# A hybrid decoder layer on one core: other distances between the steps of a hand-written TensorE order

## The chip, the core and the metric

The kernel runs on one core of one Trainium2 chip. Its metric is device time in microseconds (us), the median of several runs. A core has TensorE (PE in the rows; its weight loads are PEld) for matrix products into PSUM, VectorE (DVE), ScalarE (ACT) and GpSimd (POOL) for elementwise work, and SyncE (SP), whose queue here issues every DMA.

## The reference

One layer. `h` is the RMS-normalised input (1024 tokens of 1024 channels), `p = h @ W_in` holds the columns of all branches. Branch A is dilated sliding-window attention in three head groups, merged by their softmax denominators. Branch B is RWKV-7 time mixing: eight heads of 64 channels, each with a 64 by 64 state that is updated token by token:

```python
state = (state * w_t[:, :, None, :] + sa[..., None] * b_t[:, :, None, :]
         + v_t[..., None] * k_t[:, :, None, :])
y = jnp.einsum('bhvk,bhk->bhv', state, r_t)
...
y_rwkv = (o_rwkv * jax.nn.silu(z_rwkv)) @ w_up_rwkv[l]
merged = jax.nn.sigmoid(g_attn) * y_attn + jax.nn.sigmoid(g_rwkv) * y_rwkv
out = merged @ w_out[l]
x = x + rms_norm(out, post_norm_gain[l])
```

## The kernel before

Large products are made of three fp32r products each (high by high, high by low, low by high half). The program has four stages: `start` (normalise and transpose the input), `rwkv` (the recurrence), `attention` and `finish`.

In `rwkv` the tokens are cut into 8 segments of 128, each of two chunks of 64, and the heads into 4 pairs. For each segment there are four pieces of work, written as generators that stop (`yield`) between steps:

- `rwkv_prep` (11 steps): load and shift k and r; **wa**, the product of the low-rank codes (`pg<-wa,waup`), then the decay on DVE (`sig`, a scan into `c`); **hs,q**, the squared norms of k (`pg<-hs,q`), then `rn` on DVE (L549) and a power on POOL (L550); the **rn transpose** on PE (`pg<-ident,rn`), copied by DVE into `rt` (L560); **selp** (`pg<-rt,selp`), which spreads `rt` again, read by DVE (`kk`, L573); two steps of **ar,bk** products (`pg<-ar,bk`, 64 rows each), masked into `gt` by DVE (L597). After the second, `rwkv_blocks` writes the 16 by 16 diagonal blocks to DRAM (`tin_d`), loads them back as `xinv`, and inverts them on DVE: the **chain**, 28 small dependent operations of L624 and L626. Its result goes to DRAM (`x_d<-xinv`, four DMAs) and comes back as `xd` (`xd<-x_d`, two DMAs), and DVE transposes it into **xt** (L646). Four steps of small products (`pi`, the first three of them also followed by DVE or ACT work) then finish the inverse.
- `rwkv_rows` (3 steps): two transposes of `bw`, and `v` with `r,blk`.
- `rwkv_chain` (6 steps, C in the tables): per chunk hop 1 (`rhs<-uv,gt`, `rhs<-state,ar`, copied to `rhs_s`), hop 2 (`upd<-rhs_s,tt`, copied to `uv` by DVE L731 and ACT L732) and hop 3 (`snew<-uv,bkt`, `rhs<-uv,gt`, added to the state by DVE L738). This is the recurrence proper: each hop needs the one before.
- `rwkv_post` (2 steps): group norm and output.

Between these steps PE is given **fill**: products of projections that the rest of the program needs (`acc<-hh,whi` and its like), taken from one iterator: the second half of r/k/v, the RWKV gate (`z_chunks`), the merge gate of branch B, and the first EARLY of the 8 tiles of the other merge gate. A step of fill is one 512-column product, or two of 256 columns while r/k/v last. The other tiles of that gate are computed in `finish`.

The order of PE in this stage is fixed by hand (`keep_in_program_order`, L145). PROLOGUE is a list of (step, steps of fill behind it), where "0", "1", "2" are the preparations of the first three segments and "f" the rows of the first. LOOP is the list for one segment i: C is the chain, `t` the last step of the preparation of segment i, `e` that of i+1 (steps 8 to 10), `a` that of i+2 (steps 2 to 7), `b` the first of i+3, `f` the rows of i+1, `h` the post of i-1; its number is multiplied by FILLS (6 for most segments). All other engines and SP have an in-order queue whose order a scheduler sets at build time from its own estimate of times; so a new order on PE also gives new orders there.

PSUM for the preparation's products (`pg`) has two buffers; `raw` (loaded k, r, v) has two.

Of the kernel before, what the change touches and what calls it, by code (L numbers as in the profile page):

```python
# [34 lines left out]
C = 64  # L35
# [3 lines left out]
HALF = 512  # L39
YB = 2  # L40
BVB = 2
EARLY = 2

PROLOGUE = (("0", 24), ("0", 10), ("0", 10), ("0", 8), ("0", 44), ("0", 4), ("0", 4), ("1", 12), ("1", 16), ("1", 12),
            ("f", 4), ("f", 4), ("1", 8), ("1", 24), ("0", 8), ("0", 8), ("0", 8), ("1", 4), ("1", 6), ("0", 6), ("2", 0),
            ("f", 8))
LOOP = (("C", 0), ("t", 0), ("f", 1), ("a", 1), ("h", 1), ("C", 0), ("f", 1), ("a", 2), ("C", 0), ("a", 1), ("h", 2),
        ("C", 0), ("a", 1), ("f", 0), ("e", 2), ("C", 2), ("a", 1), ("e", 0), ("C", 1), ("a", 1), ("e", 1), ("b", 0))  # L50
FILLS = 6 * [6] + [5, 3]
CPS = SEG // C
KAPPA = math.exp(-0.5)
# [59 lines left out]
class Kernel:  # L113
# [233 lines left out]
    def rwkv(self):  # L347
# [5 lines left out]
        with ExitStack() as ctx:  # L353
# [53 lines left out]
            for t0 in range(0, S, 512):  # L407
# [11 lines left out]
            spans, fill = self.span_chunks(0), itertools.chain(self.span_chunks(1), self.z_chunks(), (  # L419
                self.gate(d, 1) for d in range(KT)), (self.gate(d, 0) for d in range(EARLY)))  # L420
            first, fill = self.ahead(spans[:8]), self.ahead(spans[8:] + list(fill))
# [11 lines left out]
            rows = self.rwkv_rows(0)  # L433
            for g, n in PROLOGUE:
                next(rows if g == "f" else prep[int(g)])
                run(n)
            for i in range(NSEG):
# [3 lines left out]
                work = dict(t=prep[i], e=prep[i + 1], a=prep[i + 2], b=prep[i + 3], f=rows, h=post)  # L441
                for g, n in LOOP:
                    if g == "C":
# [587 lines left out]
    def finish(self):  # L1031
        nc, tc, a = self.nc, self.tc, self.a
        with ExitStack() as ctx:
# [3 lines left out]
            whole, orw = self.whole, self.orw  # L1037
            for d in range(EARLY, KT):
                for _ in self.gate(d, 0):
# [122 lines left out]
```

## Time and profile before

| | |
|---|---|
| median of 3 runs | 1431.96 us (1424.61 to 1434.63) |
| the profiled execution | 1427.3 us, of which the span 1425.5 us |
| PE busy | 1334.2 us (94% of the span) |
| DVE, ACT, POOL busy | 55%, 40%, 33% |
| recurrence, fixed order | about 97 to 540 us of the span |

A row of the timeline has: start in us, length in us, engine, line, operation, tile written and tiles read, shape, count, and in brackets how long the engine stood idle before it and what ended that. A matrix product of two fp32 operands shows twice its count. PE's ends are modelled, so the length of a product is longer than the distance to the next.

### The profile page before, as it was taken

How to read it: one execution, taken by the hardware profiler on the slowest of the kernel's cores; microseconds unless marked ns; L12 is line 12 of the kernel's file. 1: busy time of each engine (PE TensorE's matmuls, PEld its weight loads, DVE VectorE, ACT ScalarE, POOL GpSimd, SP SyncE). 2: the span in 40 equal slices, each digit the busy share in tenths (PEclk: the TensorE clock that was granted, in tenths of full speed). 3: DMA queues.
4: the chain of work that ended last, by engine and by line, in shares of the span. 5: the costliest groups of instructions: out<-in, count | busy, mean ns of one | idle time of the engine just before them, and what ended most of it. 6: DMA issues, size and time to landing. Idle time of an engine off the chain costs nothing. (4 is left out here: it accounts for less than half of the span.)

```text
span 1425.5 us, 25770 instructions
## 1 busy us (share of the span) xinstructions
PE 1334.2 (94%) x10078; PEld 1118.8 (78%) x10078; DVE 780.5 (55%) x1675; ACT 575.4 (40%) x1378; POOL 477.4 (33%) x378
## 2 busy tenths in 40 slices
PE   4998799999999999999989998999899999998997
PEld 3898799777777777888868886888678877776886
DVE  5302755656565433465686558754776577338523
ACT  4435665654665332254426433543344320003211
POOL 1335534643453333322132223222223234434300
PEclk9998899999999999999999999999999999999999
DMA  8583444323332222111131112111221145654216
GB/s 170 156 241 103 119 103 120 98 71 80 106 80 57 77 77 86 46 35 52 36 96 46 41 47 75 54 50 37 58 74 31 40 150 176 201 168 141 73 35 172
DMA packets 199230, 131.17 MB, mean 92 GB/s; under 512 B 52788, under 2 KB 179340, under 8 KB 199108
## 3 DMA queue, kind: packets, MB, share of 16 engines
q1 hardware_dynamic: 199108, 129.52, 33.0%
q8 instruction: 79, 1.29, 0.4%
q14 instruction: 43, 0.35, 0.1%
HBM read 100.31 MB, written 33.89 MB: 94 GB/s over the span
## 5 line engine op out<-in xcount | busy, mean ns | idle before, releaser
L142 PE MATMUL acc<-hh,whi 128*128 128x512 f32 (+1 forms) x1360 | 480.0, 376 | 24.8 <-DVE kl L862 10.9
L142 PE MATMUL acc<-hh,wlo 128*128 128x512 f32 (+1 forms) x1360 | 469.8, 369 | 2.0 <-POOL wlo L138 1.9
L142 PE MATMUL acc<-hl,whi 128*128 128x512 f32 (+1 forms) x1360 | 469.8, 369 | 0.0
L138 POOL TENSOR_TENSOR wlo<-wstage,whi 128x512 fp32r<-128x512 f32 x186 | 250.8, 1349 | 532.2 <-DVE whi L135 262.2
L142 PEld LDWEIGHTS acc<-hh,whi 128*128 128x128 f32 x1360 | 247.7, 192 | 70.8 <-issue 16.9
L142 PEld LDWEIGHTS acc<-hh,wlo 128*128 128x128 f32 x1360 | 247.6, 192 | 41.1 <-POOL wlo L138 3.7
L142 PEld LDWEIGHTS acc<-hl,whi 128*128 128x128 f32 x1360 | 247.5, 192 | 35.3 <-issue 1.7
L882 ACT ACTIVATE L<-L,nm 128x128 f32<-128x128 f32 (+1 forms) x192 | 83.9, 438 | 84.6 <-DVE nm L879 84.4
L876 DVE CUSTOM_DVE_ANT_0 L<-pw,bias 128x128 f32<-128x128 f32 (+1 forms) x192 | 62.4, 350 | 51.6 <-PE pw L875 51.1
L861 POOL CAST k<-k 64x512 fp32r<-64x512 f32 x48 | 47.4, 988 | 107.0 <-ACT k L860 98.4
L135 DVE CAST whi<-wstage 128x512 fp32r<-128x512 f32 x108 | 53.2, 494 | 50.7 <-PE acc L142 32.3
L860 ACT CAST k<-acc 64x512 fp32r<-64x512 f32 x48 | 42.9, 894 | 75.4 <-DVE kl L862 51.9
L137 ACT CAST whi<-wstage 128x512 fp32r<-128x512 f32 x78 | 48.4, 621 | 61.0 <-PE acc L142 28.8
L852 ACT ACTIVATE q<-acc 64x512 fp32r<-64x512 f32 x48 | 43.9, 914 | 57.8 <-DVE q L853 28.6
L862 DVE TENSOR_TENSOR kl<-acc,k 64x512 fp32r<-64x512 f32 x48 | 45.7, 952 | 33.8 <-ACT k L860 33.4
L624 DVE TENSOR_TENSOR xtmp<-xinv 64x14 f32<-64x14 f32 (+6 forms) x112 | 33.5, 299 | 44.4 <-DMA xinv<-tin_d 41.5
L853 DVE SCALAR_TENSOR_TENSOR q<-acc,q 64x512 fp32r<-64x512 f32 x48 | 44.8, 933 | 20.9 <-ACT q L852 20.1
L952 ACT CAST ph<-pw 128x512 fp32r<-128x512 f32 x72 | 40.8, 583 | 36.0 <-PE pv L961 19.4
L953 DVE TENSOR_TENSOR pl<-pw,ph 128x512 fp32r<-128x512 f32 x72 | 47.2, 670 | 11.7 <-ACT ph L952 10.4
L875 PE MATMUL pw<-kl,q 128*128 128x128 f32 (+1 forms) x192 | 50.6, 278 | 1.4 <-DVE kl L862 1.4
L1102 PE MATMUL acc<-wo,mh 128*128 128x512 f32 x128 | 49.8, 389 | 0.0
L1103 PE MATMUL acc<-wo,mh 128*128 128x512 f32 x128 | 49.8, 389 | 0.0
(229 smaller groups left out, 2173.3 us busy)
## 6 DMA issues: line engine op xcount, KB each, us to landing
wstage<-in_w_in_dram SPq DMA_DIRECT2D x170, 256.0 KB
x<-in_x_dram SPq DMA_DIRECT2D x32, 256.0 KB
raw<-raw_d SPq DMA_DIRECT2D x24, 258.0 KB
raw_d<-rv SPq DMA_DIRECT2D x24, 256.0 KB
wb<-wd SPq DMA_DIRECT2D x24, 256.0 KB
bias_d<-bias_r SPq DMA_DIRECT2D x24, 192.0 KB
tb_d<-tb SPq DMA_DIRECT2D x16, 256.0 KB
ga_d<-tb SPq DMA_DIRECT2D x16, 256.0 KB
```

Of the source, the lines that this page charges most:

```text
L135: self.nc.vector.tensor_copy(hi, x)
L137: self.nc.scalar.copy(hi, x)
L138: self.nc.gpsimd.tensor_tensor(lo, x, hi.bitcast(F32), ALU.subtract)
L142: ins = self.nc.tensor.matmul(*args, **kw)
L861: nc.gpsimd.tensor_copy(self.gview(ks2[h][b], g, half), hi.bitcast(F32))
L862: nc.vector.tensor_tensor(self.gview(kl[h][a], g, half), pv, hi.bitcast(F32), ALU.subtract)
L875: nc.tensor.matmul(ps[:, :w], qs2[h][:, qc], kl[h][:, kc], start=False, stop=True)
L876: nc.vector.tensor_tensor_reduce(l[:, l0:l0 + w], ps[:, :w], self.bias[h][:, bo:bo + w], 1.0, -3.0e38, ALU.add, ALU.max, st[:, gi, 0, h, n ...
L882: nc.scalar.activation(ls, ls, AF.Exp, bias=nm[:, n:n + 1], scale=1.0, accum_out=st[:, gi, 1, h, n:n + 1])
L953: nc.vector.tensor_tensor(pl[:, :cw], ps[:, :cw], ph[:, :cw].bitcast(F32), ALU.subtract)
L1102: nc.tensor.matmul(ps, mh[k][:, ts], wh[:, k], start=k == 0, stop=False)
L1103: nc.tensor.matmul(ps, mh[k][:, ts], wl[:, k], start=False, stop=False)
```

## The change

Three tables of numbers change. EARLY goes from 2 to 3, so one more tile of the second merge gate is in the fill of the recurrence and one fewer is in `finish` (48 products of 512 columns). PROLOGUE spends 268 steps of fill instead of 232, at other places. LOOP spends the same 18 units per segment in another order, and moves `wa` in front of the first `bw`, `ar,bk` in front of `pi`, the second `ar,bk` directly behind hop 3, and the load of `b` ahead.

```diff
-EARLY = 2
+EARLY = 3
...
-PROLOGUE = (("0", 24), ("0", 10), ("0", 10), ("0", 8), ("0", 44), ("0", 4), ("0", 4), ("1", 12), ("1", 16), ("1", 12),
+PROLOGUE = (("0", 40), ("0", 16), ("0", 12), ("0", 8), ("0", 32), ("0", 8), ("0", 8), ("1", 24), ("1", 14), ("1", 12),
...
-        ("C", 0), ("a", 1), ("f", 0), ("e", 2), ("C", 2), ("a", 1), ("e", 0), ("C", 1), ("a", 1), ("e", 1), ("b", 0))
+        ("C", 0), ("a", 1), ("f", 1), ("e", 1), ("C", 0), ("b", 1), ("a", 0), ("e", 2), ("C", 0), ("a", 1), ("e", 2))
```

TensorE in the loop, segment 3, from the first chunk's hop 2 to the rn transpose (the fill between is left out). Before:

```order
L142 MATMUL upd<-rhs_s,tt_436 64x64 x8
L148 MATMUL pg<-ident,bw 128x128 x4
...
L142 MATMUL pg<-hs,q 128x2 x4
...
L142 MATMUL snew<-uv,bkt 64x64 x8
L142 MATMUL rhs<-uv,gt_432 64x64 x8
L148 MATMUL pg<-ident,rn 8x128
```

And now:

```order
L142 MATMUL upd<-rhs_s,tt_436 64x64 x8
...
L148 MATMUL pg<-ident,bw 128x128 x4
...
L142 MATMUL pg<-hs,q 128x2 x4
...
L142 MATMUL snew<-uv,bkt 64x64 x8
L142 MATMUL rhs<-uv,gt_432 64x64 x8
...
L148 MATMUL pg<-ident,rn 8x128
```

Each "..." is six steps of fill, but twelve between hs,q and snew before. From the segment's first hop to the rn transpose there are 36 steps of fill before and 42 now; from the rn transpose to selp 18 and now 12.

VectorE at the same place, from the end of the chain of L624 and L626 on. Before:

```order
L624 TENSOR_TENSOR xtmp<-xinv 64x14
L626 TENSOR_TENSOR xinv<-xinv,xtmp 64x14
L549 TENSOR_SCALAR rn<-pg 128x8
L493 SCALAR_TENSOR_TENSOR zt<-zt,acc 128x512
L556 COPY wc<-q 128x8
L738 TENSOR_TENSOR state<-snew,sw 128x256
L560 COPY rt<-pg 8x128
L646 STREAM_TRANSPOSE xt<-xd 128x512
```

And now:

```order
L624 TENSOR_TENSOR xtmp<-xinv 64x14
L626 TENSOR_TENSOR xinv<-xinv,xtmp 64x14
L731 COPY uv<-upd 64x4x64
L646 STREAM_TRANSPOSE xt<-xd 128x512
L549 TENSOR_SCALAR rn<-pg 128x8
L556 COPY wc<-q 128x8
L738 TENSOR_TENSOR state<-snew,sw 128x256
L560 COPY rt<-pg 8x128
```

The transpose of `xd`, which comes back from DRAM after the chain, stood behind `rn`, `state` and `rt`; now it stands ahead of them, and so does the copy `uv` stand behind the chain (before, seven of its operations came after `uv`). The same turn, xt ahead of rn, is in the queue in segments 0 to 4; in segment 5 rn stays ahead, and segments 6 and 7 have no rn.

VectorE in the prologue, around the rn and rt of the second preparation. Before:

```order
L626 TENSOR_TENSOR xinv<-xinv,xtmp 64x5x10
L549 TENSOR_SCALAR rn<-pg 128x8
L624 TENSOR_TENSOR xtmp<-xinv 64x54
...
L624 TENSOR_TENSOR xtmp<-xinv 64x14
L626 TENSOR_TENSOR xinv<-xinv,xtmp 64x14
L560 COPY rt<-pg 8x128
```

And now:

```order
L624 TENSOR_TENSOR xtmp<-xinv 64x44
L549 TENSOR_SCALAR rn<-pg 128x8
L626 TENSOR_TENSOR xinv<-xinv,xtmp 64x11x4
...
L624 TENSOR_TENSOR xtmp<-xinv 64x14
L626 TENSOR_TENSOR xinv<-xinv,xtmp 64x14
L560 COPY rt<-pg 8x128
```

Here `rt` stays behind the whole chain, and `rn` moves from behind 10 of its 28 operations to behind 21. On PE there are 86 steps of fill between the second ar,bk of the first preparation and the selp of the second, instead of 60.

The attention stage has the same order on every engine as before; in `finish` one gate tile is gone from PE, DVE, POOL and SP, and nothing else is moved on PE.

## Rows read from the trace of the kernel before

**Rows 1.** The page's part 1: busy us (share), instructions; PE alone.

```profile
PE 1334.2 (94%) x10078; PEld 1118.8 (78%) x10078; DVE 780.5 (55%) x1675; ACT 575.4 (40%) x1378; POOL 477.4 (33%) x378
```

**Rows 2.** Waits of PE, 0 to 560 us: releaser, us in total, times, longest.

```profile
PE pg L142 <- ACT q L542: 8.6, 2, 5.8
PE pg L148 <- POOL rn L550: 7.6, 6, 1.9
PE pg L142 <- DVE rt L560: 5.4, 1, 5.4
PE pg L142 <- DVE kk L573: 2.2, 2, 1.9
...
PE snew L142 <- ACT uv L732: 0.9, 2, 0.6
```

**Rows 3.** Timeline of PE in the prologue, 100 to 166 us.

```profile
112.52 1.87 PE L142 MATMUL pg<-hs,q 128*128 128x2 f32 x8 [5.76 <-ACT q L542]
...
115.25 0.63 PE L142 MATMUL acc<-hh,wlo 128*128 128x256 f32 x2
...
149.27 0.94 PE L142 MATMUL pg<-hs,q 128*128 128x2 f32 x7 [2.81 <-ACT q L542]
...
165.66 2.07 PE L142 MATMUL pg<-rt,selp 8*128 8x128 f32 x8 [5.35 <-DVE rt L560]
```

**Rows 4.** Busy time by stretch, the prologue: engines, then granted clock, DMA share, GB/s.

```profile
97.00:195.00 98.00, 83.62 (x929) 79.28 (x929) 42.49 (x89) 54.18 (x129) 48.19 (x39) 0.90 0.46 119
```

**Rows 5.** Timeline of DVE in segment 3 of the loop.

```profile
348.75 0.17 DVE L624 TENSOR_TENSOR xtmp<-xinv 64x14 f32<-64x14 f32 x1 [3.99 <-DMA xinv<-tin_d]
...
360.33 0.18 DVE L626 TENSOR_TENSOR xinv<-xinv,xtmp 64x14 f32<-64x14 f32 x1
360.43 0.15 DVE L549 TENSOR_SCALAR rn<-pg 128x8 f32<-128x8 f32 x1
...
367.60 0.71 DVE L646 STREAM_TRANSPOSE xt<-xd 128x512 f32<-128x512 f32 x1 [3.52 <-DMA xd<-x_d]
```

**Rows 6.** Timeline of PE in segment 3: hop 1, hop 3, rn transpose.

```profile
344.02 1.11 PE L142 MATMUL rhs<-uv,gt 64*128 64x64 f32 x16
...
359.57 0.69 PE L142 MATMUL snew<-uv,bkt 128*64 128x64 f32 x16
...
362.34 0.27 PE L148 MATMUL pg<-ident,rn 128*8 128x128 f32 x1 [1.47 <-POOL rn L550]
```

**Rows 7.** SP's DMA issues behind the chain of segment 2.

```profile
310.77 1.80 SPq L629 DMA_DIRECT2D x_d<-xinv  x4
313.94 1.28 SPq L644 DMA_DIRECT2D xd<-x_d  x2
```

**Rows 8.** Segment 0: PE's rn transpose, then DVE's xt and rt.

```profile
212.25 0.27 PE L148 MATMUL pg<-ident,rn 128*8 128x128 f32 x1 [0.97 <-POOL rn L550]
...
214.97 0.71 DVE L646 STREAM_TRANSPOSE xt<-xd 128x512 f32<-128x512 f32 x1 [4.33 <-DMA xd<-x_d]
...
215.92 0.26 DVE L560 COPY rt<-pg 8x128 f32<-8x128 f32 x1
```

**Rows 9.** Timeline of PE: a 64-row product alone among fill.

```profile
132.62 0.40 PE L142 MATMUL acc<-hl,whi 128*128 128x256 f32 x2
132.94 1.21 PE L142 MATMUL pg<-ar,bk 64*64 64x64 f32 x64
134.08 0.51 PE L142 MATMUL acc<-hh,wlo 128*128 128x256 f32 x2
134.43 0.41 PE L142 MATMUL acc<-hh,whi 128*128 128x256 f32 x2
134.67 0.41 PE L142 MATMUL acc<-hl,whi 128*128 128x256 f32 x2
```

**Rows 10.** Waits of PE in the last stage, 1100 to 1426 us.

```profile
PE acc L142 <- DVE tb L467: 6.3, 4, 2.8
```

**Rows 11.** What DVE waited for before L646, whole span: us, times.

```profile
  DMA xd<-x_d: 32.3, 8
```

More of the change, by code (lines that the diff above doesn't have):

```diff
@@ L41 @@
 BVB = 2
-EARLY = 2
-PROLOGUE = (("0", 24), ("0", 10), ("0", 10), ("0", 8), ("0", 44), ("0", 4), ("0", 4), ("1", 12), ("1", 16), ("1", 12),
-            ("f", 4), ("f", 4), ("1", 8), ("1", 24), ("0", 8), ("0", 8), ("0", 8), ("1", 4), ("1", 6), ("0", 6), ("2", 0),
+EARLY = 3
+PROLOGUE = (("0", 40), ("0", 16), ("0", 12), ("0", 8), ("0", 32), ("0", 8), ("0", 8), ("1", 24), ("1", 14), ("1", 12),
+            ("f", 4), ("1", 20), ("f", 4), ("1", 16), ("0", 8), ("0", 8), ("0", 8), ("1", 6), ("1", 6), ("0", 6), ("2", 0),
             ("f", 8))
-LOOP = (("C", 0), ("t", 0), ("f", 1), ("a", 1), ("h", 1), ("C", 0), ("f", 1), ("a", 2), ("C", 0), ("a", 1), ("h", 2),
-        ("C", 0), ("a", 1), ("f", 0), ("e", 2), ("C", 2), ("a", 1), ("e", 0), ("C", 1), ("a", 1), ("e", 1), ("b", 0))
+LOOP = (("C", 0), ("t", 0), ("a", 1), ("f", 1), ("h", 1), ("C", 1), ("f", 1), ("a", 1), ("C", 1), ("a", 1), ("h", 1),
+        ("C", 0), ("a", 1), ("f", 1), ("e", 1), ("C", 0), ("b", 1), ("a", 0), ("e", 2), ("C", 0), ("a", 1), ("e", 2))
 FILLS = 6 * [6] + [5, 3]
```

## The prediction

> **What bounds the kernel now.** I read the busy shares first. TensorE is busy 94% of the span [rows 1], and the change adds and removes no product, so only the time in which PE stands still, or runs at the lower clock, can change: 91 us of standing in all. The waits of PE up to the end of the recurrence come next [rows 2]: 8.6 us for `q`, 7.6 for `rn` in six waits, 5.4 for `rt`, 2.2 for `kk`, 0.9 for `uv`. The timeline of the prologue [rows 3] shows that `q` and `rt` are three long waits: 5.76, 2.81 and 5.35 us, 13.9 together. Behind such a wait products are slower: a pair of 256 columns takes 0.63 us at 115.25 [rows 3] against 0.40 at 132.62 [rows 9], and the granted clock is 0.90 over these 98 us [rows 4]. If that is a mix of the two levels, 1.2 and 2.4 GHz, about 20 us ran at the lower one, which loses at most 9.8 us. Part of the 20 us was standing anyway; I take 7.3, or 2.4 per long wait, with 0 and 3.3 as ends. Last I read the loop: what VectorE does between the chain, `rn` and `xt` [rows 5, 8], where that lies against PE's steps [rows 6], and what SP does meanwhile [rows 7].
>
> **The prologue.** All distances here are in fill steps of 0.24 us: so far apart do undisturbed pairs start, 134.43 to 134.67 [rows 9]. First wait: from the loads to hs,q there are 22 more steps (16 and 6), 5.3 us of the 5.76; 0.5 us stays. Second: 10 more steps from loads to hs,q, 2.4 of 2.81; 0.4 stays. Third, the selp that waits for `rt`: `rt` still stands behind the whole chain in VectorE's queue. PE now has 26 more steps before it, 6.2 us, but no longer loses the second wait and the slow clock behind it, 5.2 us, so it arrives only 1.0 us later against the chain: 4.3 us stay, split between `rn`, which has moved back to the 21st of 28 operations, and `rt`. With 2.4 us of slow clock that makes 7.6 of the 21.2 us before: **13.6 us saved**. Ends: 21.2 (all waits gone) and 0 (the chain or GpSimd's queue holds the ar,bk products up instead).
>
> **The loop, VectorE's queue.** Here the price lies. In segments 0 to 4 `xt` now stands ahead of `rn`. `xt` needs `xd`, which goes to DRAM and back after the chain's last operation: 360.51 to 367.60, 7.09 us [rows 5]. It waits for that DMA in all eight segments [rows 11]. The engine does not pass over a waiting operation: in segment 0, where `xt` already stood ahead of `rt`, PE's rn transpose was through at 212.5, yet `rt` ran at 215.92, right behind `xt` [rows 8]. And PE's rn transpose waits for `rn` and the power on GpSimd: 360.43 to 362.34, 1.91 us [rows 5, 6].
>
> For one segment, in us after its hop 1 (344.02 [rows 6]): the chain runs from 4.73 to 16.49 [rows 5]. Its ar,bk now comes six steps sooner before the next hop 1, up to 1.4 us, but the masks stay behind `state` and the norm's sums on VectorE; I take 0.9, so it ends at 15.6. `xd` is back at 22.7, `xt` done at 23.4, and the rn transpose can start at 25.3. PE arrives there at 18.32 less the 1.47 it waited, plus six steps (1.4) and one more change of product shape (0.2): 18.4. **It waits 6.9 us**, where it waited 1.5. The copy `uv`, now behind the chain, holds hop 3 until 16.0 against an arrival near 15.6; that is inside the 6.9. The wait is long like the three of the prologue, so 2.4 us of slow clock follow. Segment 0 from its own rows: `xt` done at 215.68, transpose at 217.6, arrival 212.25 less 0.97 plus 1.6, so 4.7 and 2.4 [rows 8]. Segment 5 keeps `rn` ahead, and with 12 more steps between ar,bk and `rn` waits nothing.
>
> Sum: 4 x (6.9 + 2.4) + 7.1 = 44.3, less the 7.6 and 0.9 of before [rows 2]: **35.8 us lost**. Ends: if the chain ends 3 us sooner and no clock falls, 4 x 3.9 + 2 - 8.5 = 9; if it ends 2 us later, with 3.3 us of clock, 4 x 12.2 + 8 - 8.5 = 48. Behind the waiting `rn` stand `wc`, `state` and `rt`. `state` is wanted at the next hop 1, twelve steps behind the transpose, and is done before the transpose: no further wait. From the rn transpose to selp there are six steps fewer, 1.4 us, so `kk` may be late for r,blk; the slow fill there gives these steps back, and I leave `kk` at 2.2.
>
> By the Trainium skill, DMA: Bandwidth & Descriptors, Anatomy of one DMA, a DMA costs about 2 us whatever its size; two in turn would be 4.0 us, an estimate, and the wait 3.8 instead of 6.9. The trace speaks against stopping there: between the two landings SP also issues, 1.80 and 1.28 us [rows 7], which is the missing 3.1; the row's 7.09 stands.
>
> **Shapes side by side.** A 64-row product alone among fill costs 0.32 - 0.24 us on entry and 0.35 - 0.24 on exit, 0.2 together [rows 9]. Each loop pass has two such groups fewer (wa behind `pi`, ar,bk before `pi` and behind hop 3, against pi now apart from r,blk): 0.4 us. But four 128-row steps (two `bw`, rn, r,blk) stood next to a hop or `pi` and now have a change of their own, about 0.1 each. Zero, with 3 us either way over the eight segments.
>
> The Trainium skill, TensorEngine Tiling (Array Packing), Key Properties, says that a change of tiling mode drains the engine. These rows agree that it costs something, but by it the order would be a gain only if changes went away, and they mostly move.
>
> **The gate tile.** 48 products leave the last stage and 36 steps enter the prologue, 12 the end of the recurrence, at about 0.24 us: nothing, to 0.4 us. In the last stage four waits for `tb` [rows 10] come from VectorE's other work; the tile that goes stands behind them, so I leave them. If that cover is gone, the next stage's first products meet VectorE's work earlier: 3 us at most, the longest of these waits.
>
> **Sum.** 1427.3 - 13.6 + 35.8 + 0.4 = 1449.9: **1450 us**. The profiled execution is 4.7 us below the median of the runs, 1431.96, so the same sum against the median would be 1454; both are in the range.
>
> **Rivals.**
> - *The two halves meet* (0.18): the chain ends three or four us sooner, because sooner `wa` takes `sig` and the scan out of its way, and no clock falls. Loss 9 to 20, prologue -13.6: about 1430. For it, 3.99 us of idle time before the chain [rows 5]; against it, the trip of `xd`, which nothing shortens. A trip of 4.0 us would give 5 x 3.1 = 15.5 less, 1434, the same case.
> - *The prologue gives nothing* (0.14): GpSimd's order or `rn` makes new waits as long as the old ones. 1427.3 + 35.8: 1463.
> - *Faster* (0.08): the loop's wait does not grow. The chain's loads land early, while PE is in hop 1, and it ends within 10 us of that hop; then `xt` is done at 17.8 and the transpose waits 1.3 us, as today. Each us later costs 5. With all 21.2 us of the prologue saved, and the loop as before or a little worse (+5): 1411. For it, VectorE idles for these loads; against it, they wait for two DMAs of their own that the change leaves alone.
> - *Nothing moves* (0.04): PE's longer waits fall where other engines would have stopped it anyway: 1427.
>
> The forecast has 0.56, its own range 1438 to 1462. With the first two rivals, and the ends of the prologue and the loop, 1428 to 1468 leaves out 0.2: the fast side mostly. A measurement of this kernel tells about 1% (14 us) from no change. Above 1446 lie 0.48 of the forecast and the second rival's 0.14: slower 0.62. Same: 0.08 of the forecast, 0.16 of the first rival, 0.04: 0.28. Faster 0.10.
>
> **What would show it.** In the trace after: five waits of PE's rn transpose of 5 to 8 us each in segments 0 to 4, none in segment 5; VectorE idle 5 us or more before `xt`, with `rn` directly behind; a granted clock below 1.0 in those segments; in the prologue no wait of 3 us for `q`, and one of some 4 us for `rn` or `rt`. Wrong would be: `rn` waits of 2 us or less (then the chain or the trip was misjudged), a prologue still at 0.90, or a last stage longer by over 3 us.

## The result, and the profile after

The changed kernel takes 1445.4 us (median of 6 runs, 1441.5 to 1449.4) against 1426.0 for the kernel before on the same chip (six runs, among them the three behind the 1431.96 of the table above): a ratio of 1.0124, with an interval from 1.0101 to 1.0147. The loss is clear of the noise, but small. The profiled run has a span of 1444.3 us, 18.8 more than before.

PE was busy for about as long as before and stood still more [rows 1]:

```profile
PE 1339.4 (93%) x10078; PEld 1120.2 (78%) x10078; DVE 767.7 (53%) x1673; ACT 578.6 (40%) x1380; POOL 477.7 (33%) x378
```

Where the time went is read from marks on PE, the same instructions in both traces: the first hop 1 of segment 0, that of segment 6, and the last hop of the recurrence; then the first product of the attention stage that has to wait. Before (timeline of PE):

```profile
194.87 1.11 PE L142 MATMUL rhs<-uv,gt 64*128 64x64 f32 x16
...
488.01 1.11 PE L142 MATMUL rhs<-uv,gt 64*128 64x64 f32 x16
...
543.87 0.69 PE L142 MATMUL snew<-uv,bkt 128*64 128x64 f32 x16
...
568.82 0.47 PE L142 MATMUL acc<-hh,whi 128*128 128x512 f32 x1 [2.52 <-DVE q L853]
```

After, with segment 3 between them (its hop 1, first bw, rn transpose and post transpose, with what PE waited for in brackets):

```profile
191.89 1.11 PE L142 MATMUL rhs<-uv,gt 64*128 64x64 f32 x16
...
356.80 1.11 PE L142 MATMUL rhs<-uv,gt 64*128 64x64 f32 x16
...
365.55 0.66 PE L148 MATMUL pg<-ident,bw 128*128 128x128 f32 x4 [2.88 <-ACT sig L530]
...
381.44 0.37 PE L148 MATMUL pg<-ident,rn 128*8 128x128 f32 x1 [3.36 <-POOL rn L550]
381.47 0.78 PE L142 MATMUL acc<-hh,whi 128*128 128x512 f32 x1
...
384.18 0.86 PE L148 MATMUL pg<-ident,d 128*128 128x128 f32 x4
...
518.93 1.11 PE L142 MATMUL rhs<-uv,gt 64*128 64x64 f32 x16
...
574.83 0.69 PE L142 MATMUL snew<-uv,bkt 128*64 128x64 f32 x16
...
600.49 0.47 PE L142 MATMUL acc<-hh,whi 128*128 128x512 f32 x1 [0.53 <-DVE q L853]
```

- Prologue: the first hop comes 3.0 us sooner, with 36 more fill steps of 0.24 us ahead of it (8.6): 11.6 us saved in this pair of traces.
- Segments 0 to 5, the same fill in both: 293.1 us before, 327.0 after: **33.9 us lost**.
- Segments 6 and 7, the same fill in both: 55.9 us in both.
- From the last hop to the end: 881.6 and 869.5, 12.1 less. 48 products have left `finish`, and 12 of them run behind the last hop (102 products up to the wait of the last row, 90 before), so 36 products of 0.24 us are 8.6 of it: **3.5 saved**. 2.0 of that is the first wait of the attention stage, 2.52 us before and 0.53 after: the 12 steps cover it.

Together that makes +18.8 us. What ended PE's waits in the loop (190 to 580 us of after; releaser, us in total, times, longest):

```profile
PE pg L148 <- ACT sig L530: 13.9, 5, 3.9
PE pg L148 <- POOL rn L550: 13.5, 5, 4.1
PE pg L142 <- DVE kk L573: 4.0, 2, 2.2
PE pi L142 <- DVE xq L652: 3.6, 3, 2.1
```

The wait for `rn` grew from 7.6 to 13.5 us [rows 2], but as much went to a waiter that was not there before: the bw transposes wait for `sig`. VectorE in the same segment 3 (in brackets its idle time and what ended it):

```profile
361.05 0.17 DVE L624 TENSOR_TENSOR xtmp<-xinv 64x14 f32<-64x14 f32 x1 [6.67 <-DMA xinv<-tin_d]
...
363.12 0.68 DVE L756 TENSOR_TENSOR d<-yt,sm 128x512 f32<-128x512 f32 x1
...
371.56 0.17 DVE L626 TENSOR_TENSOR xinv<-xinv,xtmp 64x14 f32<-64x14 f32 x1
371.65 0.41 DVE L731 COPY uv<-upd 64x256 f32<-64x256 f32 x1
378.91 0.71 DVE L646 STREAM_TRANSPOSE xt<-xd 128x512 f32<-128x512 f32 x1 [6.85 <-DMA xd<-x_d]
379.55 0.13 DVE L549 TENSOR_SCALAR rn<-pg 128x8 f32<-128x8 f32 x1
```

And ScalarE:

```profile
363.83 0.63 ACT L757 ACTIVATE yt<-d 128x512 f32<-128x512 f32 x1 [3.61 <-DVE d L756]
364.37 1.13 ACT L530 ACTIVATE sig<-pg,vecs 128x128 f32<-128x128 f32 x4
```

The lower half is the forecast: 6.85 us of idle time before `xt`, and `rn` directly behind it, where it ran right behind the chain before [rows 5]. The upper half is the same pattern twice in a row: the chain's first operation waits for its load, the post's `d` stands behind it on VectorE, `yt` waits for `d` on ScalarE, and `sig` stands behind `yt`. `wa` now comes ahead of the first bw and has filled both `pg` buffers; until `sig` has read one, the bw transpose can't start.

The granted clock, [rows 4] and a stretch of segment 1, the loop's slowest segment (busy time by stretch of after; the number behind the five engines is the clock):

```profile
97.00:195.00 98.00, 91.45 (x1052) 87.02 (x1051) 39.50 (x97) 57.07 (x134) 52.93 (x42) 0.95 0.48 128
...
245.00:295.00 50.00, 43.35 (x476) 34.79 (x474) 27.61 (x68) 25.56 (x66) 20.07 (x16) 0.90 0.28 74
```

### The profile page after: what moved, and what is told of

Same layout as the page of the kernel before. It is cut to its first block, busy times and chain, and to the rows that moved or that the text cites. A ratio compares the mean times of both kernels' runs of the same rounds, so it can differ in the third digit from the quotient of the medians.

```text
span 1444.3 us, 25775 instructions
## 1 busy us (share of the span) xinstructions
PE 1339.4 (93%) x10078; PEld 1120.2 (78%) x10078; DVE 767.7 (53%) x1673; ACT 578.6 (40%) x1380; POOL 477.7 (33%) x378
## 5 line engine op out<-in xcount | busy, mean ns | idle before, releaser
L142 PE MATMUL acc<-hh,whi 128*128 128x512 f32 (+1 forms) x1360 | 485.3, 380 | 23.9 <-DVE kl L862 11.3
L135 DVE CAST whi<-wstage 128x512 fp32r<-128x512 f32 x106 | 53.0, 501 | 46.8 <-PE acc L142 27.9
L624 DVE TENSOR_TENSOR xtmp<-xinv 64x14 f32<-64x14 f32 (+6 forms) x112 | 29.2, 261 | 46.3 <-DMA xinv<-tin_d 43.7
```

Source lines behind the costliest of these rows:

```text
L135: self.nc.vector.tensor_copy(hi, x)
L142: ins = self.nc.tensor.matmul(*args, **kw)
```

## The experiments

Theory: the transpose `xt`, which waits for the trip of `xd`, stands ahead of `rn`, and sets when PE gets through the rn transpose; the wait for `sig` lies inside the same stretch and only takes some of it over. Rival: two separate causes whose prices add. The first three runs change VectorE's or ScalarE's queue; PE's order in all of them is that of the changed kernel. Each edit is a pin: `issue_after` puts one instruction behind another in its engine's queue, and the scheduler orders the rest around it. A ratio compares with the kernel before run beside the same experiment on the same chip, where its median lay between 1427.5 and 1430.4 us; between experiments the ratios are the safer comparison. 1445.4 us is a ratio of 1.0124.

**E1: xt behind rt again (segments 1 to 6).**

```diff
-        nc.vector.tensor_copy(rt, ps[0:n, 1])
+        self.rt_at = nc.vector.tensor_copy(rt, ps[0:n, 1])
...
-        nc.vector.transpose(flat(dt), flat(d))
...
+        if not 1 <= sg["s"] <= 6: nc.vector.transpose(flat(dt), flat(d))
...
+        if 1 <= sg["s"] <= 6:
+            with self.tc.issue_after(self.rt_at.ins): nc.vector.transpose(flat(dt), flat(d))
```

> The changed kernel (1445.4 us), with only one thing different: on VectorE the transpose xt of segments 1 to 6 stands behind rn, state and rt again. Theory (the trip of xd ahead of rn is what PE waits for): PE's rn transpose finds rn ready about 17.3 us after hop 1 (chain end 14.9, uv, rn, power 1.9) and arrives later than that, held up by the waits for sig, so the 13.5 us of rn waits in the loop go, with some 5 us of slow clock; the 13.9 us for sig stay: 1427 us. Rival (the chain itself, not the trip, makes rn late): rn waits of 1.5 us or more stay in each segment and the time is 1436 or more. Other rival: xt is now late for pi, a new wait of the same size: 1440 or more.

Measured 1426.0 us, a ratio of 0.997 (0.995 to 0.999). The waits for `rn` in the loop are gone altogether, those for `sig` stay (190 to 580 us, first rows):

```profile
PE pg L148 <- ACT sig L530: 14.7, 5, 4.1
PE pi L142 <- DVE xq L652: 4.4, 5, 1.6
```

Up to the last hop nothing but `xt` has another place in the queues of VectorE, ScalarE and GpSimd than in the changed kernel. So the trip, not the chain, made `rn` late, and `pi` has room for the later `xt`.

**E2: sig ahead of yt (segments 1 to 5), xt left ahead of rn.**

```diff
-                nc.scalar.activation(dst[:, p], ps[:, p], AF.Tanh, bias=col(b0, p), scale=0.5)
+                self.aa_at = nc.scalar.activation(dst[:, p], ps[:, p], AF.Tanh, bias=col(b0, p), scale=0.5)
...
-        nc.scalar.activation(yt, dh, AF.Square)
+        with self.tc.issue_after(self.aa_at.ins): nc.scalar.activation(yt, dh, AF.Square)
```

> The changed kernel, with only the post's square yt (L757) put behind sig and aa (L530) in ScalarE's queue in segments 1 to 5; xt stays ahead of rn. Theory (one bound for the stretch from hop 1 to the rn transpose: chain, then xd, then rn, 24.4 us): the five waits for sig, 13.9 us, go, but the rn waits grow by as much in segments 1 to 4, from 11.0 to some 21 us; only segment 5, which has rn ahead, keeps its 3.9 us: 1439 to 1442 us. Rival (two causes that add): the rn waits stay at 13.5 and the time falls by 13.9 and 4 to 6 us of slow clock, to about 1426.

Measured 1444.3 us against 1445.4, a ratio of 1.009 (1.006 to 1.011) against 1.0124: 1 us faster by the medians, 5 by the ratios, where the intervals overlap. The waits for `sig` are gone; others took their place:

```profile
PE pg L148 <- POOL rn L550: 16.6, 5, 4.3
PE pg L142 <- ACT bkt L688: 4.8, 3, 2.6
PE pi L142 <- DVE xq L652: 3.9, 4, 2.1
PE pg L142 <- DVE kk L573: 2.9, 3, 1.5
PE pg L142 <- DVE rt L560: 1.2, 1, 1.2
```

The rival, which asked for some 19 us, is out. The time is 2 us above the theory's range: part of the room went to hs,q, which waits for `bkt`, and segment 5, where `xt` stands ahead of `rt` instead of `rn`, still takes 50.6 us.

**E3 and E11: both edits.**

> Both edits in one: xt behind rt, sig ahead of yt. Theory: no wait for sig, rn waits of about 1 us per segment as in the kernel before, the loop at some 293 us for segments 0 to 5 instead of 327: 1410 to 1414 us, below the kernel before (1426) by what the prologue saved. Rival (the order on PE itself costs, shapes or clock): the waits go but the loop keeps 10 us or more of the loss: 1422 or more.

> Both pins again, beside the third and the kernel before on the same chip: 1411 us, 0.983 to 0.989 of the kernel before. If the third pin is worth its 3.5 us it lies above it by 2 to 4 us.

Measured 1411.2 us (ratio 0.986, 0.983 to 0.989) and, on another chip, 1413.2 (0.990, 0.987 to 0.993, a little above what I had expected of the repeat): below both kernels. Segments 0 to 5 take 292.9 us in the first trace, as before the change. The same edit as E2 that bought 1 to 5 us alone buys 11 to 16 us here (1426.0 to 1411.2 and 1413.2; by the ratios 0.011 and 0.008): most of the wait for `sig` counts only once the wait for `rn` is gone. Left in the loop of E3:

```profile
PE pi L142 <- DVE xq L652: 4.2, 5, 2.1
PE pg L142 <- ACT bkt L688: 3.5, 3, 1.7
PE pg L142 <- DVE kk L573: 2.7, 3, 1.1
```

**E5: the kernel before, with xt pinned ahead of rn.**

```diff
-        nc.vector.tensor_scalar(rn, ps[:, 0, 0:n], 1e-24, None, ALU.max)
+        with self.tc.issue_after(self.xt_at[s - 1].ins) if 2 <= s <= 6 else ExitStack(): nc.vector.tensor_scalar(rn, ps[:, 0, 0:n], 1e-24, None, ALU.max)
...
-        nc.vector.transpose(flat(dt), flat(d))
+        self.xt_at = {**getattr(self, "xt_at", {}), sg["s"]: nc.vector.transpose(flat(dt), flat(d))}
```

> The kernel before (all its tables), with one thing different: on VectorE the transpose xt of the preceding preparation is put ahead of rn in segments 0 to 4, as it stands in the changed kernel; PE's order is the same. Theory (the price per segment as it was predicted): rn is through on GpSimd 26.2 us after hop 1 (chain end 16.5, xd 7.1, xt 0.7, power 1.9), PE arrives at 16.9: five waits of rn of 6 to 9 us, 43 us in all instead of 7.3, and 2.4 us of slow clock each: 1470 to 1478 us against 1428. Rival (the long wait costs little beyond its growth, and the later segments give part of it back): waits of 4 us and 1445 to 1455.

Measured 1473.5 us (ratio 1.032, 1.028 to 1.036). The waits (191 to 560 us), and a segment of it with its clock:

```profile
PE pg L148 <- POOL rn L550: 49.0, 6, 10.9
```

```profile
247.00:306.00 59.00, 47.96 (x647) 41.09 (x647) 28.71 (x71) 28.87 (x73) 25.47 (x21) 0.88 0.33 75
```

With PE's order untouched, the turn of `xt` and `rn` on VectorE costs 46 us. The scheduler moved other work with it (on ScalarE L743 and L513, on GpSimd the power L550), so the price is that of the turn with what followed from it. Segments 0 to 5 grew by 46.8 us and all of PE's waits in them by 39.8 (those for `rn` by 41.4), so the lower clock and the rest cost some 7 us, about 1.4 per long wait, not 2.4. The total came out inside the range I gave because two items missed it in opposite ways: the five waits came to 47.5 us instead of 43 (the trip took 8.7 us in segment 1), the clock to less.

**E4 and E8: the parts.** E4 has the new PROLOGUE and EARLY = 3 with the old LOOP; E8 has the old PROLOGUE and EARLY = 2 with the new LOOP and both edits.

```diff
-LOOP = (("C", 0), ("t", 0), ("a", 1), ("f", 1), ("h", 1), ("C", 1), ("f", 1), ("a", 1), ("C", 1), ("a", 1), ("h", 1),
...
+LOOP = (("C", 0), ("t", 0), ("f", 1), ("a", 1), ("h", 1), ("C", 0), ("f", 1), ("a", 2), ("C", 0), ("a", 1), ("h", 2),
...
```

E8 against E3:

```diff
-EARLY = 3
+EARLY = 2
...
-PROLOGUE = (("0", 40), ("0", 16), ("0", 12), ("0", 8), ("0", 32), ("0", 8), ("0", 8), ("1", 24), ("1", 14), ("1", 12),
...
+PROLOGUE = (("0", 24), ("0", 10), ("0", 10), ("0", 8), ("0", 44), ("0", 4), ("0", 4), ("1", 12), ("1", 16), ("1", 12),
...
```

> EARLY = 3 and the new PROLOGUE with the old LOOP. Theory: the prologue's saving of 11.6 us and the gate tile at nothing, the loop as before: 1414 us against 1426 of the kernel before. Rival (the prologue moves the scheduler's order in the loop too, or its waits come back in segment 0): 1420 or more.

> Both pins with the new LOOP, but the old PROLOGUE and EARLY = 2. Theory (prologue and loop add): the 11.6 us that the new prologue saved are lost again: 1423 us. Rival (what the prologue saves is given back in segment 0, or the old one's waits don't matter here): 1411 to 1416.

E4: 1416.9 us, ratio 0.990 (0.988 to 0.992), about 14 us saved and 3 us above the theory's 1414. E8: 1419.1 us, 0.994 (0.991 to 0.996); against the same kernel with the new prologue (E3, E11) that puts EARLY and the prologue together at 0.004 to 0.008 of the time, 6 to 12 us; 1419.1 lies between the theory's 1423 and the rival's 1416. The saving is real and adds to the loop's, but it is not the prologue's alone: with EARLY = 2 the attention stage has its first wait of 2.5 us (here and in E5 as in the kernel before), with the new tables 0.5 to 0.8.

**E6, E7, E9: can the order be had without pins, or made better?** E6 puts `wa` behind the first bw again and pins `xt` as in E1. E7 is E3 with the second `pi` six steps later. E9 is E3 with the exponentials L554 and L555 behind the copies `bkt` on ScalarE.

```diff
-LOOP = (("C", 0), ("t", 0), ("a", 1), ("f", 1), ("h", 1), ("C", 1), ("f", 1), ("a", 1), ("C", 1), ("a", 1), ("h", 1),
+LOOP = (("C", 0), ("t", 0), ("f", 1), ("a", 1), ("h", 1), ("C", 1), ("f", 1), ("a", 1), ("C", 1), ("a", 1), ("h", 1),
```

```diff
-        ("C", 0), ("a", 1), ("f", 1), ("e", 1), ("C", 0), ("b", 1), ("a", 0), ("e", 2), ("C", 0), ("a", 1), ("e", 2))
+        ("C", 0), ("a", 1), ("f", 1), ("e", 1), ("C", 0), ("b", 2), ("a", 0), ("e", 1), ("C", 0), ("a", 1), ("e", 2))
```

```diff
-        nc.scalar.activation(ewm, cm, AF.Exp, scale=-0.5 * KAPPA)
-        nc.scalar.activation(ei, c, AF.Exp, scale=0.5 * KAPPA)
+        with self.tc.issue_after(self.bkt_at.ins) if s >= 2 else ExitStack(): nc.scalar.activation(ewm, cm, AF.Exp, scale=-0.5 * KAPPA)
+        with self.tc.issue_after(self.bkt_at.ins) if s >= 2 else ExitStack(): nc.scalar.activation(ei, c, AF.Exp, scale=0.5 * KAPPA)
...
-            nc.scalar.copy(bkt[halves[0], :, 0, ch], ps[halves[1], :, 0:HD])
+            self.bkt_at = nc.scalar.copy(bkt[halves[0], :, 0, ch], ps[halves[1], :, 0:HD])
```

> The changed kernel with wa behind the first bw again (its old place on PE) and xt behind rt; ScalarE's order is left to the scheduler. Theory: with wa behind the first bw no bw transpose waits for the PSUM buffer that sig has to empty, so the 13.9 us for sig go without any pin on ScalarE, and the rn waits with xt: as with both pins, 1408 to 1414 us. Rival (the waits for sig come from sig being late on ScalarE, wherever wa stands): the second bw or hs,q waits for sig instead, 8 us or more in all, 1420 or more.

> Both pins (1411 us), and in LOOP one unit of fill moved from behind the second pi to behind the load b, so that the second pi comes six steps later. Theory: the five waits of pi for xq, 4.2 us, go: 1406 to 1408 us. Rival (it moves the wait to the third or fourth pi, or to snew behind it): 1410 to 1413.

> Both pins, and a third: ScalarE's two exponentials of the decay (L554, L555), which wait for GpSimd and the scan on VectorE, behind the copies bkt of both bw in segments 0 to 5. Theory (again a queue's head that waits for another engine, with a copy behind it that frees a PSUM buffer): the three waits of hs,q for bkt, 3.5 us, go, nothing else: 1407 to 1409 us where both pins alone give 1411. Rival (the exponentials come later, so wc, ar and bk come later and kk or arbk take the wait over): 1411 to 1416.

E6: 1418.0 us (0.993, 0.991 to 0.996): the waits for `sig` (0.5 us left, in the prologue) and `rn` (0.2) went as expected, but one wait of `wa` for `bkt`, 4.2 us in segment 1, and 9.7 us for `xq`, `kk` and `uv` came; 4 us above the range I gave. E7: 1415.6 (0.991, 0.987 to 0.994): the `xq` waits are gone and those for `bkt` grew from 3.5 to 7.5. E9: 1412.6 against 1413.2 for E11 beside it: the same. Its waits in the loop:

```profile
PE pg L142 <- DVE kk L573: 5.9, 4, 1.7
PE pi L142 <- DVE xq L652: 5.0, 4, 2.1
PE pg L148 <- POOL rn L550: 2.3, 2, 1.3
PE snew L142 <- ACT uv L732: 1.6, 2, 0.8
```

In E9 the rival was right. In E7 neither side was: the wait came back at hs,q, which the rival did not name, and the time is 3 us above the rival's range. Both times a wait of 3 or 4 us taken away came back elsewhere.

**E10: EARLY = 3 alone.**

```diff
-EARLY = 2
+EARLY = 3
```

> The kernel before with EARLY = 3 alone: one gate tile leaves the last stage, its 48 products come at the end of the recurrence's fill. Theory (a product costs 0.24 us in either place): 1426 to 1429 us against 1427.5, no change. Rival (its cover is gone, and the next stage starts later or its waits for tb grow): 3 us slower.

Measured 1422.7 us, ratio 0.9955 (0.9934 to 0.9976), a little faster: both expectations missed. One part shows in the trace. All 48 products run behind the last hop here, and the first wait of the attention stage, 2.5 us in each of the three traces with EARLY = 2, is gone; from the last hop to the end the run takes 879.5 us instead of 881.6, though the waits for `tb` grew from 6.3 us [rows 10] to 8.0.

The other difference is in the prologue, whose tables did not change: the wait for `rt` fell from 5.4 us [rows 3] to 0.7, and the first hop came at 189.64 instead of 194.87. That is not shown to be EARLY's doing. Up to the first hop VectorE, ScalarE, GpSimd and SP have the same order in this trace as in the kernel before; and E5 and E8, whose tables there are the old ones too, waited 0.7 and 1.9 us for `rt` and came to the first hop at 191.68 and 192.65. The long wait for `rt` stands in one of four traces (the last section shows how it comes about). In the profiled run 4.6 of the 5.2 us went again in segments 0 to 5. What the rest of the 0.0045 comes from stays open.

## Why the prediction was right, and where it was not

The time (1450 forecast, 1445 measured), the sign and the main mechanism hold; the items inside the sum were not all as I had them. I gave 0.62 to a time above 1446 us; 1445.4 lies just below that line, 1% above the median of 1431.96, while the loss of 1.2% against 1426.0 is more than the 1% that I had taken as the least that can be told.

- *The stretch from hop 1 to the rn transpose.* I had the transpose possible 25.3 us after hop 1; in segment 3 it came at 24.6 (356.80 to 381.44), in segments 1 to 4 at 23.6 to 25.0. Chain end (15.6 forecast, 14.9 measured), trip (7.09; 7.18 here) and power (1.91; 1.89 here) were right. In segment 0 it came at 20.5 instead of 22.7.
- *"PE arrives there at 18.4; it waits 6.9 us"*: **this step failed.** PE arrived at 21.3, because it had waited 2.9 us for `sig` at the bw transpose, and stood 3.4 for `rn`. I counted six steps and a change of shape for its way and did not ask, of the step that moves (`wa`), who empties the two buffers it fills and behind what that reader stands in ScalarE's queue. The total came out nearly right because both waits lie in one stretch with one end: E2 shows it, where the first goes and the time falls by 1 to 5 us only. Part of it is luck: segments 0 to 4 lost 29.5 us where the sum has about 36, and segment 5, which it has at nothing, lost 4.4. The sign that I named against the theory, waits for `rn` of 2 us or less, came up in two segments (1.92 and 1.61) although chain and trip were nearly as forecast: waits for `sig` of 2.64 and 1.97 us stood ahead of them in the same stretch.
- *"Segment 5 waits nothing"* failed for the same reason: `rn` was in time, but `sig` cost 3.9 us there and the segment grew by 4.4.
- *The slow clock, 2.4 us per long wait*, was mis-sized. In segments 0 to 5 PE's waits grew by 24.3 us (35.0 against 10.7) and the time by 33.9: 9.6 us for the clock and the shapes, over some 13 waits of 1.5 us or more. It differs from wait to wait: behind the 3.36 us in segment 3 six steps took 2.7 us instead of 1.5 (381.47 to 384.18, at a granted clock of 0.50, the lower level); behind the 2.88 us in the same segment twelve steps took 0.24 us each, at 1.00.
- *The prologue, 13.6 saved*: 11.6 in this pair of traces. Single traces are a poor measure of it: the first hop came at 189.6 to 194.9 us in the four traces with the old PROLOGUE, at 186.7 to 193.7 in the nine with the new one. By the means, 192.2 and 191.1, and the 8.6 us of added fill, about 10 us are saved, and the 5.35 us for `rt`, a quarter of the 21.2, were 0.7 to 1.9 us in the other three old ones. The waits for `q` are gone. I left 4.3 us at one wait for `rn` or `rt` and 0.9 at `q`; measured were `rn` 2.0 and 3.3, and 1.2 for `rv`, and a clock of 0.95 instead of 0.90.
- *The gate tile* at +0.4 measured -3.5 from the last hop on, though the waits for `tb` grew to 7.4 us from 6.3 [rows 10]. I asked what its products cover in the stage that they leave, and not what they cover where they go: the first wait of the attention stage.
- *The 2 us of a DMA* is given by the Trainium skill, DMA: Bandwidth & Descriptors, Anatomy of one DMA, as the fixed part for a DMA issued by GpSimd, with the time of the data on top; SP issues the DMAs here, and no row here times one of them alone. The sum went by the row, 7.09 us, and not by this.
- Of the rivals, the two halves do not meet, and the prologue does give its saving. The one that ended faster asked for `xt` to be done 17.8 us after hop 1; it was at 22.8 (378.91 and 0.71, less 356.80).

The sum again with measured terms, on the span: -11.6 + 33.9 - 3.5 = +18.8; forecast was -13.6 + 35.8 + 0.4 = +22.6.

## What to carry to other kernels

When a hand-written order on one engine moves, read the queues of the others at the same place: an instruction that waits for a DMA holds everything behind it, and through a second engine's queue and a small ring of buffers it can stop PE at a step that has nothing to do with the DMA. Waits that lie in one stretch with one end do not add: removing the first alone gave 1 to 5 us (E2), the last alone about 20 (E1), both about 35 (E3, E11). And a wait that one trace shows may be that execution's: look whether a second trace of the same order has it before you count on removing it. The remedy here was two pins, one on VectorE and one on ScalarE, and with them the change is a gain of 1 to 1.5% over the kernel before.

## What the runs showed of the hardware that was not expected

The 5.35 us wait for `rt` in the prologue of before [rows 3] comes from a meeting of VectorE and GpSimd. The chain ahead of `rt` there, from the timeline of VectorE, and GpSimd beside it:

```profile
159.10 0.21 DVE L624 TENSOR_TENSOR xtmp<-xinv 64x50 f32<-64x50 f32 x1
159.34 1.25 DVE L626 TENSOR_TENSOR xinv<-xinv,xtmp 64x50 f32<-64x50 f32 x1
160.62 1.30 DVE L624 TENSOR_TENSOR xtmp<-xinv 64x44 f32<-64x44 f32 x1
```

```profile
159.23 1.29 POOL L566 TENSOR_TENSOR k<-k,c 128x512 f32<-128x512 f32 x1 [0.23 <-ACT c L565]
160.60 1.26 POOL L567 TENSOR_TENSOR bk<-k,sig 128x512 f32<-128x512 f32 x1
```

In E10, with the same order on VectorE, GpSimd's `k` comes later, and the same operations are short:

```profile
159.10 0.21 DVE L626 TENSOR_TENSOR xinv<-xinv,xtmp 64x50 f32<-64x50 f32 x1
159.35 0.20 DVE L624 TENSOR_TENSOR xtmp<-xinv 64x44 f32<-64x44 f32 x1
```

```profile
160.48 1.32 POOL L566 TENSOR_TENSOR k<-k,c 128x512 f32<-128x512 f32 x1 [1.71 <-ACT c L565]
```

A chain operation of 0.2 us took 1.2 to 1.3 when a GpSimd operation of 1.3 us had started beside it. Of the 224 chain operations of the kernel before, 26 took over 0.6 us, all of them beside a GpSimd operation on tiles of 256 or 512 columns; 6 more overlapped such an operation by over 0.1 us and stayed short; of the other 192 none was long. The Trainium skill, SBUF — State Buffer, SBUF: two separate sides, says that a VectorE operation with two SBUF inputs and a GpSimd operation that reads SBUF share a pair of ports under an exclusive lock, and that the loser is blocked until the other ends. The rows agree for the wide operations: the long ones end with GpSimd's. They do not for GpSimd's power on 128x8 elements, shown as 1.64 us long, beside which at least 24 chain operations kept their 0.2 us.

The chain of the second preparation lasted 17.7 us before and 14.6 in E10. It ended 3.4 us sooner there, and PE came 1.3 us later to the selp, which is the 4.7 us by which the wait for `rt` differs. What moved `k` is TensorE, not the program. Behind the wait for `q` PE reached the first bw transpose at 154.65 us before and at 155.89 in E10: the granted clock was 0.50 from 149.1 to 155.5 us in E10, and 0.68 from 149.3 to 154.6 before. ScalarE, in the same order in both, waited for PE in E10 only:

```profile
156.09 0.62 ACT L137 CAST whi<-wstage 128x512 fp32r<-128x512 f32 x1 [1.49 <-PE acc L142]
```

Behind this cast stands `c`, which lets `k` start. So in one execution TensorE came back to its full clock sooner, GpSimd's `k` started into the chain, and TensorE stood for `rt` longer than it had gained.
